# Rotary query columns of four heads in one tile, in a two-layer hybrid decoder kernel

## The chip, the cores and the metric

The kernel runs on one core of one Trainium2 chip. The metric is device time in microseconds (us), the median of the runs shown; one execution was also recorded by the hardware profiler, and all durations below come from that one. TensorE is written PE, its weight loads PEld, VectorE DVE, ScalarE ACT, GpSimd POOL, and SyncE, which issues most transfers, SP.

## The reference, cut to what matters

Two layers work on a residual stream of 512 tokens by 1024 features. Each projects it into an S5 branch, a multi-head latent attention (MLA), a memory cross-attention, gates and a merge. The change lies in MLA, whose query is built like this:

```
q = (_rms_norm(c_q, q_norm) @ w_uq).reshape(bsz, s, 8, 64 + 32)
q_nope = q[..., :64]
q_rope = _apply_rope(q[..., 64:], cos, sin)      # t1*cos - t2*sin | t1*sin + t2*cos
k_rope = _apply_rope(k_rope_in[:, :, None, :], cos, sin)[:, :, 0, :]   # one key for all heads
sc = einsum(q_nope, k_nope) + einsum(q_rope, k_rope), scaled by 96 ** -0.5
p = softmax(where(causal, sc, neg));  out = p @ v
```

c_q has 256 features, there are 8 heads, and each head has 64 plain and 32 rotary features, of which the first 16 (t1) are rotated with the last 16 (t2).

## The kernel before, in words

Everything is held transposed, features on the 128 partitions and the 512 tokens along the row. A product of two fp32 operands is three matmuls: each operand is split into a high part rounded to fp32r and the rest (`split_to`, lines 606 to 610: ACT writes the high part, DVE the low one), and `mm3` (lines 97 to 99) adds high by high, high by low and low by high into one PSUM tile. A weight block is loaded by SP, split the same way, and held in a ring of 4. PSUM has three tiles under the tag "mm" for such products, one under "tp" for transposes, two under "sc" for scores.

PE runs in an order written out by hand; generators hand it pieces of work. The other engines each run in order too, with instructions placed by a scheduler. `attention` walks over the heads. For each it makes the next head's inputs (`prepare`), four score tiles of 128 queries (`mla_scores`, each followed by mask, maximum, exponential, sum and scaling on DVE and ACT), and, delayed by four tiles, the values of the head before (`mla_values`: transposes of the probabilities, a copy of them out of PSUM, two matmuls). Between these pieces PE runs "fill": projections, the GLU and merge products that have nothing to do with attention. Each score tile is followed by 2.5 us of the planner's time of other work, taken from the next head's inputs and the fill (`lace` gives each yield of the inputs 1.2 us of fill). The fill of an even head is queued when that head begins; when the queue is empty PE gets none.

Per pair of heads `mla_k` makes the plain keys, and copies the shared rotated key (32 rows) into each head's key tile, on POOL (line 935). Per head `mla_q` (lines 942 to 958) makes one 128-row PSUM tile: 64 plain features, 32 rotary features, and the same 32 again with t1 and t2 exchanged. So a head has 2 x 3 matmuls of 512 columns. Then ACT copies the plain rows out (line 950), DVE multiplies rows 64 to 95 by the cosines, rows 96 to 127 by the signed sines, and adds (lines 951 to 953), and ACT and DVE split the 96 rows (lines 609, 610). The scores contract over 96 rows.

The cosine table is made in layer 0 during the first merges (`rope_tables`, `v_sincos`), turned by four transposes on PE (line 360) and copied out of PSUM by DVE (line 361). `rotary_sums` and `rotate_key` rotate the shared key right behind it, and in layer 1 at the start of the layer.

Of the kernel before, what the change touches and what calls it, by code (L numbers as in the profile page):

```python
# [230 lines left out]
def const_setup(E):  # L231
# [7 lines left out]
    g.tensor_tensor(out=E.sel[:, 0:32], in0=E.ident[:, 0:32], in1=E.ident[:, 32:64], op=ALU.add)
    for o in (64, 96):  # L240
        g.tensor_tensor(out=E.sel[:, 0:32], in0=E.sel[:, 0:32], in1=E.ident[:, o:o + 32], op=ALU.add)
    g.tensor_copy(E.sel[:, 32:48], E.sel[:, 16:32])
    g.tensor_copy(E.sel[:, 48:64], E.sel[:, 0:16])
# [92 lines left out]
def rope_tables(E):  # L336

    nc, cst = E.nc, E.cst
    v = nc.vector
# [8 lines left out]
    rt = R("rt", 512).rearrange("p (t f) -> p t f", t=4)  # L348
    s3 = rsn.rearrange("p (t f) -> p t f", t=4)
    c3 = rcs.rearrange("p (t f) -> p t f", t=4)  # L350
    for o in range(0, 128, 64):
        v.tensor_copy(rt[:, :, o:o + 16], c3)
        v.tensor_copy(rt[:, :, o + 16:o + 32], c3)
        v.tensor_scalar(out=rt[:, :, o + 32:o + 48], in0=s3, scalar1=-1.0, scalar2=None, op0=ALU.mult)
        v.tensor_copy(rt[:, :, o + 48:o + 64], s3)
# [1139 lines left out]
```

## Time and profile before

| | |
|---|---|
| median of 3 runs | 1108.19 us (1103.96, 1108.19, 1113.60) |
| the profiled execution, its own time | 1108.54 us |
| its span, first to last instruction | 1106.6 us |
| granted PE clock, mean over the span | 0.99 |
| PE / PEld busy | 95% / 77% |
| DVE / ACT / POOL busy | 63% / 46% / 45% |
| share of the last chain: PE / DVE / DMA / ACT / issue | 73% / 11% / 6% / 4% / 4% |

A matmul's listed length reaches past the start of the next one, because matmuls overlap; what a matmul takes out of PE's time is the distance from its start to the next start. A number in brackets at a row's end is the idle time of that engine before it, and what ended it. Layer 0's MLA stretch is 296 to 460 us, layer 1's 830 to 990 us.

### The profile page before, as it was taken

To read this page: it belongs to the slowest core of one execution; us is meant where nothing else is said; L and a number is where in the kernel's file an instruction comes from. 1 tells how busy PE (TensorE), PEld (TensorE's weight loads), DVE (VectorE), ACT (ScalarE), POOL (GpSimd) and SP (SyncE) were. 2 spreads that over 40 slices of the span, in tenths; PEclk is the share of its full clock that TensorE was granted. 3 is DMA by queue.
4 is the path that set the end of the run, shared out by engine and by line. 5 is a ranking of instruction groups with operands and counts; after the bars stand their busy time and mean duration, and the time that the engine had idled before them with its cause. 6 is when DMAs were issued, how large, how long until landed. Compare 5 with 4: busy or idle time off the path is not lost.

```text
span 1106.6 us, 16062 instructions
## 1 busy us (share of the span) xinstructions
PE 1054.7 (95%) x5584; PEld 846.8 (77%) x5584; DVE 693.4 (63%) x1275; ACT 509.5 (46%) x1013; POOL 496.2 (45%) x889
## 2 busy tenths in 40 slices
PE   8939998999999999999989999999999999999996
PEld 6638886887876777788878788888888777778885
DVE  7596869747575654764396675864547665545427
ACT  5315553333566665333335356434347656543331
POOL 3998965871042333682570075673002333310163
PEclk9979999999999999999999999999999999999999
DMA  6515243453321222344545344254432212234342
GB/s 200 176 39 134 81 120 94 120 134 103 100 84 51 61 66 67 115 134 131 150 145 165 110 100 119 83 133 111 114 103 88 74 51 69 75 105 133 101 148 77
DMA packets 87666, 117.97 MB, mean 107 GB/s; under 512 B 24097, under 2 KB 36513, under 8 KB 87585
## 3 DMA queue, kind: packets, MB, share of 16 engines
q1 hardware_dynamic: 86944, 114.85, 36.0%
q0 software_dynamic: 640, 2.10, 0.6%
q8 instruction: 44, 0.72, 0.3%
q14 instruction: 38, 0.30, 0.1%
HBM read 107.37 MB, written 9.55 MB: 106 GB/s over the span
## 4 chain that ended last, share of the span: by engine, by line
PE 73%; DVE 11%; DMA 6%; ACT 4%; issue 4%; POOL 1%; SPq 0%; DVEq 0%; ACTq 0%; POOLq 0%
PE mm L97 20%; PE mm L99 20%; PE mm L98 20%; DVE w L607 3%; PE av L990 2%; DMA raw<-in_w_mem_kv 2%; PE tp L982 2%; ACT w L606 1%; PE pb L519 1%; DMA yd<-r 1%; PE py L543 1%; DMA yb<-yd 1%; PE sa L98 1%; DMA raw<-in_xT 1%; PE sa L99 1%
## 5 line engine op out<-in xcount | busy, mean ns | idle before, releaser
L97 PE MATMUL mm<-X,w 128*128 128x512 f32 x740 | 298.0, 403 | 2.3 <-ACT w L606 1.4
L607 DVE TENSOR_TENSOR w<-raw,w 128x512 fp32r<-128x512 f32 (+1 forms) x247 | 216.4, 881 | 122.9 <-ACT w L606 121.6
L99 PE MATMUL mm<-X,w 128*128 128x512 f32 x740 | 289.4, 391 | 0.1
L98 PE MATMUL mm<-X,w 128*128 128x512 f32 x740 | 289.0, 391 | 0.0
L606 ACT CAST w<-raw 128x512 fp32r<-128x512 f32 (+1 forms) x317 | 191.3, 607 | 183.7 <-PE mm L99 80.1
L71 POOL TENSOR_TENSOR w<-raw,w 128x512 fp32r<-128x512 f32 x70 | 92.7, 1326 | 339.6 <-ACT w L606 259.8
L97 PEld LDWEIGHTS mm<-X,w 128*128 128x128 f32 x740 | 139.7, 189 | 32.1 <-issue 2.8
L99 PEld LDWEIGHTS mm<-X,w 128*128 128x128 f32 x740 | 139.0, 188 | 31.1 <-DVE w L607 0.8
L98 PEld LDWEIGHTS mm<-X,w 128*128 128x128 f32 x740 | 139.4, 188 | 26.4 <-DVE X L607 0.2
L99 PE MATMUL mm<-hl,w 128*128 128x512 f32 (+1 forms) x296 | 110.4, 373 | 18.1 <-DVE w L607 18.1
L97 PE MATMUL mm<-hl,w 128*128 128x512 f32 (+1 forms) x296 | 112.0, 378 | 0.2
L98 PE MATMUL mm<-hl,w 128*128 128x512 f32 (+1 forms) x296 | 109.7, 371 | 0.3 <-DVE hl L610 0.3
L99 PEld LDWEIGHTS mm<-hl,w 128*128 128x128 f32 x296 | 56.8, 192 | 28.5 <-DVE w L607 19.3
L97 PEld LDWEIGHTS mm<-hl,w 128*128 128x128 f32 x296 | 57.1, 193 | 9.7 <-DVE z L727 1.1
L98 PEld LDWEIGHTS mm<-hl,w 128*128 128x128 f32 x296 | 56.9, 192 | 9.2 <-DVE hl L610 1.0
L1048 ACT ACTIVATE thg<-mm,bg 128x512 f32<-128x512 f32 x48 | 32.9, 686 | 62.1 <-PE mm L99 61.8
L782 ACT ACTIVATE P<-P,mx 128x256 f32<-128x256 f32 (+2 forms) x96 | 51.1, 542 | 12.2 <-DVE mx L781 12.2
L780 ACT ACTIVATE P<-sa,mx 128x128 f32<-128x128 f32 (+1 forms) x64 | 33.7, 527 | 31.2 <-DVE mx L772 30.6
L1058 DVE SCALAR_TENSOR_TENSOR thg<-thg,mm 128x512 f32<-128x512 f32 x32 | 22.0, 688 | 34.0 <-PE mm L99 33.2
L777 DVE TENSOR_TENSOR sa<-sa,mask 128x128 f32<-128x128 f32 x64 | 19.1, 298 | 35.0 <-PE sa L99 34.3
L935 POOL TENSOR_SCALAR hl<-hl 32x512 fp32r<-32x512 f32 x32 | 21.1, 658 | 43.1 <-PE mm L98 28.5
L71 POOL TENSOR_TENSOR macc<-macc,thg 128x512 f32<-128x512 f32 x16 | 22.5, 1405 | 36.7 <-DVE thg L1058 36.6
(364 smaller groups left out, 1986.2 us busy)
## 6 DMA issues: line engine op xcount, KB each, us to landing
raw<-in_w_in SPq DMA_DIRECT2D x188, 256.0 KB
raw<-in_p SPq DMA_DIRECT2D x48, 256.0 KB
raw<-in_w_mem_kv SPq DMA_DIRECT2D x32, 256.0 KB
raw<-in_w_out SPq DMA_DIRECT2D x32, 256.0 KB
tz<-kd SPq DMA_DIRECT2D x8, 512.0 KB
raw<-in_w_glu SPq DMA_DIRECT2D x16, 256.0 KB
raw<-in_xT SPq DMA_DIRECT2D x8, 256.0 KB
raw<-in_memT SPq DMA_DIRECT2D x8, 256.0 KB
```

The source lines that it names most:

```text
L71: ins = g.tensor_tensor(**k)
L97: t.matmul(out, lhsT=a[0], rhs=b[0], start=start, stop=False)
L98: t.matmul(out, lhsT=a[0], rhs=b[1], start=False, stop=False)
L99: t.matmul(out, lhsT=a[1], rhs=b[0], start=False, stop=stop)
L606: nc.scalar.copy(hi, src)
L607: (eng or nc.vector).tensor_tensor(out=lo, in0=src, in1=fl(hi), op=ALU.subtract)
L780: nc.scalar.activation(out=P, in_=ps, func=AF.Exp, bias=mx[:, 1:2], accum_out=mx[:, 2:3])
L782: nc.scalar.activation(out=P, in_=P, func=AF.Copy, scale=mx[:, 3:4])
L982: nc.tensor.transpose(tp[:, cols(t)], Ps[t][:, cols(kb)], E.ident)
L990: mm = lambda out, rhs, start, stop: nc.tensor.matmul(out, lhsT=w, rhs=rhs, start=start, stop=stop)
L1048: nc.scalar.activation(out=th, in_=pg, func=AF.Tanh, bias=E.bg2[:, col:col + 1], scale=0.5)
L1058: v.scalar_tensor_tensor(out=th, in0=th, scalar=1.0, in1=pp, op0=ALU.add, op1=ALU.mult)
```

## The change

The doubled 32 columns per head go. The columns of `w_uq` are ordered anew: for four heads (a "quad") one tile of 128 rotary rows, t1 of heads a and b, t2 of heads a and b, then the same for c and d; and for each pair of heads one tile of 2 x 64 plain rows. So a quad has 3 tiles where it had 4, and `mla_q_rope` and `mla_q` run 18 matmuls where 24 ran. A score tile now contracts over 128 rows: 64 plain rows of the head and the 64 rotary rows of its pair, and the key tile holds the shared rotated key at the rows of that head and zeros at the rows of the other (`sel` is 128 columns wide for that).

`rope` rotates on DVE: four products of 32 rows by the sines, read crosswise, one product of 128 rows by the cosines, and one sum of 64 rows per pair. It yields four times, so that fill comes between. `mla_q` then makes both heads of a pair at once: each head's plain rows are split from PSUM, the pair's rotary rows are split once for the first head, and ACT copies the two parts into the second head's tiles. `mla_k` copies the key's rotary rows on ACT for the first head and on POOL for the second. The tables are now two, cosines and sines, each turned by four transposes; the single "tp" tile serves both.

```diff
-    E.sel = cst.tile([128, 64], F32, name="sel")
+    E.sel = cst.tile([128, 128], F32, name="sel")
...
 def rope_tables(E):
...
-    E.cs = cst.tile([128, 512], F32, name="cs", tag="cs")
-    tp = E.psum.tile([128, 512], F32, name="tp", tag="tp", bufs=E.cfg["tp"])
-    for t in range(4):
-        nc.tensor.transpose(tp[:, t * 128:t * 128 + 128], rt[:, t, :], E.ident)
-    nc.vector.tensor_copy(E.cs, tp)
+    E.cs = []
+    for r, tag in ((rc, "cs"), (rs, "sin")):
+        tp = E.psum.tile([128, 512], F32, name="tp", tag="tp", bufs=E.cfg["tp"])
+        for t in range(4):
+            nc.tensor.transpose(tp[:, t * 128:t * 128 + 128], r[:, t * 128:t * 128 + 128], E.ident)
+        E.cs.append(cst.tile([128, 512], F32, name="cs", tag=tag))
+        nc.vector.tensor_copy(E.cs[-1], tp)
...
+def rope(E, a, b, ps, outs):
+    v = E.nc.vector
+    cos, sin = E.cs
+    for o in (0, 32, 64, 96):
+        i = o ^ 32
+        v.tensor_tensor(out=b[o:o + 32, :], in0=ps[i:i + 32, :], in1=sin[i:i + 32, :], op=ALU.mult)
+        if o == 32:
+            yield
+    yield
+    v.tensor_tensor(out=a, in0=ps, in1=cos, op=ALU.mult)
+    for r, out in outs:
+        v.tensor_tensor(out=out, in0=a[r, :], in1=b[r, :], op=ALU.add)
+        yield
...
         for i in range(2):
-            nc.gpsimd.tensor_scalar(out=k[i][64:96, :], in0=fl(E.kr[i][64:96, :]), scalar1=1.0, scalar2=0.0,
-                                    op0=ALU.mult, op1=ALU.add)
+            if j:
+                nc.gpsimd.tensor_scalar(out=k[i][64:128, :], in0=fl(E.kr[i][64:128, :]), scalar1=1.0, scalar2=0.0,
+                                        op0=ALU.mult, op1=ALU.add)
+            else:
+                nc.scalar.copy(k[i][64:128, :], fl(E.kr[i][0:64, :]))
...
-def mla_q(E, l, hp, j, wq):
-    pq = pmm(E)
-    for k in range(2):
-        mm3(E, pq, wq.at(cols(2 * j + k)), E.cn[k].at(ALL), k == 0, k == 1)
-    qf, tb = ftile(E, "qf"), ftile(E, "qb")
-    nc.scalar.copy(qf[0:64, :], pq[0:64, :])
-    v.tensor_tensor(out=qf[64:96, :], in0=pq[64:96, :], in1=E.cs[64:96, :], op=ALU.mult)
-    v.tensor_tensor(out=tb[64:96, :], in0=pq[96:128, :], in1=E.cs[96:128, :], op=ALU.mult)
-    v.tensor_tensor(out=qf[64:96, :], in0=qf[64:96, :], in1=tb[64:96, :], op=ALU.add)
-    q = ftile2(E, "A")
-    split_to(E, q[0][0:96, :], q[1][0:96, :], qf[0:96, :], 96 ** -0.5)
-    yield
+def mla_q_rope(E, l, hq):
+    w = wblock(E, E.I["w_uq"][l, hq, :, 0:512])
+    pq = pmm(E)
+    for k in range(2):
+        mm3(E, pq, w.at(cols(k)), E.cn[k].at(ALL), k == 0, k == 1)
+    r = [stile(E, "qr") for _ in range(2)]
+    yield from rope(E, ftile(E, "qa"), ftile(E, "qb"), pq, [(cols(i, 64), r[i][64:128, :]) for i in range(2)])
+    return [(r[0], w), (r[1], None)]
+
+def mla_q(E, l, hp, qr, wq):
+    o = 2 if wq else 0
+    wq = wq or wblock(E, E.I["w_uq"][l, hp // 2, :, 512:768], 256)
+    pq = pmm(E)
+    for k in range(2):
+        mm3(E, pq, wq.at(cols(o + k)), E.cn[k].at(ALL), k == 0, k == 1)
+    qs = [ftile2(E, "A") for _ in range(2)]
+    r = slice(64, 128)
+    for j, q in enumerate(qs):
+        split_to(E, q[0][0:64, :], q[1][0:64, :], pq[cols(j, 64), :], 96 ** -0.5)
+        if j == 0:
+            split_to(E, q[0][r, :], q[1][r, :], qr[r, :], 96 ** -0.5)
+            yield
+        else:
+            for i in range(2):
+                nc.scalar.copy(q[i][r, :], fl(qs[0][i][r, :]))
...
         if j == 0:
             ks[hp] = yield from mla_k(E, l, hp)
-            ws[hp] = wblock(E, E.I["w_uq"][l, hp])
-        qs[h] = yield from mla_q(E, l, hp, j, ws[hp])
+            if h % 4 == 0:
+                ws[hp], ws[hp + 1] = yield from mla_q_rope(E, l, h // 4)
+            qs[h], qs[h + 1] = yield from mla_q(E, l, hp, *ws[hp])
```

The written order moves at three places that the prediction speaks of. In the rows, "waits X" says on which engine's signal an instruction waits.

First, PE in layer 0 where the tables are turned (`ident` is the unit matrix, `carve` the tables, `ks`, `sel` the shared key). Before:

```order
L894 MATMUL mm<-ks,sel 64x512 [waits DVE_49]
L360 MATMUL tp<-ident,carve 128x128 x4
L97 MATMUL mm<-X,w 128x512 [waits Activation_49]
L98 MATMUL mm<-X,w 128x512
L99 MATMUL mm<-X,w 128x512 [waits DVE_49]
```

And now:

```order
L899 MATMUL mm<-ks,sel 128x512 [waits DVE_49]
L363 MATMUL tp<-ident,carve 128x128 x4
L363 MATMUL tp<-ident,carve 128x128 [waits DVE_49]
L363 MATMUL tp<-ident,carve 128x128 x3
L97 MATMUL mm<-X,w 128x512 [waits Activation_49]
```

Four more transposes stand there, and the first of them waits for DVE, which has to copy the first four out of the one "tp" tile. On DVE that copy keeps its place, behind the scan (line 531 before) and four more instructions.

Second, DVE of the changed kernel where the fifth head's first score tile comes near (`sa` are scores, `mx` the softmax's columns, `qr` rotary rows, `hl<-mm` the plain rows of the query):

```order
L781 TENSOR_TENSOR sa<-sa,mask 128x128 [waits PE_49]
L611 TENSOR_TENSOR w<-raw,w 128x512 [waits DMAHW6_49,Activation_49]
L776 TENSOR_REDUCE mx<-sa 128x1 [waits DVE_49]
L614 SCALAR_TENSOR_TENSOR hl<-qr,hl 64x512 [waits Activation_49]
L785 RECIPROCAL mx<-mx 128x1 [waits Activation_49]
L614 SCALAR_TENSOR_TENSOR hl<-mm,hl 64x512 [waits Activation_49]
L611 TENSOR_TENSOR w<-raw,w 128x512 [waits DMAHW7_49,Activation_49]
L781 TENSOR_TENSOR sa<-sa,mask 128x128 [waits PE_49]
```

The query's last piece, `hl<-mm`, stands behind the reciprocal of the softmax of the fourth head's last tile. On PE its six matmuls now come right behind that score tile, and six matmuls of fill later the fifth head's first score tile needs them; before, a head's six matmuls stood three score tiles or more ahead of their use.

Third, PE in layer 1 at the end of the second head. Before:

```order
L97 MATMUL sa<-hl 128x512 [waits DVE_49]
L990 MATMUL av<-pt,vv 64x128 [waits Activation_49]
L982 MATMUL tp<-ident,P 128x128 [waits PE_49]
L97 MATMUL mm<-ysm,w 128x512
L98 MATMUL mm<-ysm,w 128x512
L99 MATMUL mm<-ysm,w 128x512 [waits Pool_49]
...
L97 MATMUL sa<-hl 128x128 [waits Activation_49]
L982 MATMUL tp<-ident,P 128x128 [waits Activation_49]
```

And now:

```order
L97 MATMUL sa<-hl 128x512 [waits Activation_49]
L1026 MATMUL av<-pt,vv 64x128 [waits Activation_49]
L1018 MATMUL tp<-ident,P 128x128 [waits PE_49]
L97 MATMUL sa<-hl 128x128 [waits Activation_49]
L1018 MATMUL tp<-ident,P 128x128 [waits Activation_49]
```

The twelve matmuls of fill between the two score tiles are gone from here; the four yields of `rope` have used the fill earlier. Layer 0 had no fill at this point already. At the end of each MLA stretch, too, one block of twelve fill matmuls between the last head's transposes is gone.

## Rows read from the trace of the kernel before

**Rows 1.** The page, part 1: busy time, share of the span, instructions.
```profile
PE 1054.7 (95%) x5584; PEld 846.8 (77%) x5584; DVE 693.4 (63%) x1275; ACT 509.5 (46%) x1013; POOL 496.2 (45%) x889
```
**Rows 2.** Waits of PE: engine, line, releaser; us in total, times, longest.
```profile
PE mm L99 <- DVE w L607: 18.1, 5, 12.2
PE tp L982 <- ACT P L782: 4.7, 4, 2.6
PE av L990 <- ACT pt L985: 3.5, 8, 0.7
PE tx L1123 <- DVE mv L181: 3.2, 1, 3.2
```
**Rows 3.** Timeline of PE, first and last of 38 even matmuls: start, length.
```profile
295.65 0.39 PE L98 MATMUL mm<-hl,w 128*128 128x512 f32 x1
304.04 0.39 PE L99 MATMUL mm<-hl,w 128*128 128x512 f32 x1
```
**Rows 4.** Timeline of PE at the turning of the table.
```profile
252.72 0.66 PE L360 MATMUL tp<-ident,carve 128*128 128x128 f32 x4
253.13 0.49 PE L97 MATMUL mm<-X,w 128*128 128x512 f32 x1
```
**Rows 5.** Timeline of DVE at the same place.
```profile
252.95 1.22 DVE L531 TENSOR_TENSOR_SCAN pb<-r,pb 128x512 f32<-128x512 f32 x1
...
256.21 0.69 DVE L361 COPY cs<-tp 128x512 f32<-128x512 f32 x1
```
**Rows 6.** Timeline of PE: the longer early waits.
```profile
60.80 0.58 PE L99 MATMUL mm<-hl,w 128*128 128x256 f32 x1 [4.66 <-DVE w L607]
80.40 0.58 PE L99 MATMUL mm<-hl,w 128*128 128x256 f32 x1 [12.19 <-DVE w L607]
```
**Rows 7.** Stretches: length, busy PE, PEld, DVE, ACT, POOL, then PE's granted clock.
```profile
60.00:62.00 2.00, 1.20 (x5) 1.20 (x6) 2.00 (x2) 0.00 (x0) 2.00 (x8) 0.63 0.16 25
62.00:64.00 2.00, 1.73 (x9) 1.44 (x7) 2.00 (x1) 0.59 (x1) 2.00 (x9) 0.52 0.32 107
572.00:574.00 2.00, 0.13 (x1) 0.14 (x2) 1.98 (x7) 1.71 (x4) 1.96 (x3) 1.00 0.00 0
345.00:400.00 55.00, 53.97 (x280) 40.53 (x279) 33.17 (x74) 33.00 (x77) 19.15 (x30) 1.00 0.22 64
```
**Rows 8.** Timeline of DVE, then of PE, at layer 0's first heads.
```profile
304.66 0.69 DVE L951 TENSOR_TENSOR qf<-mm,cs 32x512 f32<-32x512 f32 x1
...
310.99 1.46 DVE L1035 TENSOR_TENSOR gl<-gl,z 128x512 f32<-128x512 f32 x1
308.47 0.22 PE L97 MATMUL sa<-hl 96*128 96x128 f32 x1
324.76 0.33 PE L982 MATMUL tp<-ident,P 128*128 128x128 f32 x1 [2.59 <-ACT P L782]
```
**Rows 9.** Timeline of PE, end of the second head: layer 0, layer 1.
```profile
341.83 0.33 PE L982 MATMUL tp<-ident,P 128*128 128x128 f32 x1 [1.65 <-ACT P L782]
872.75 0.66 PE L982 MATMUL tp<-ident,P 128*128 128x128 f32 x4
```
**Rows 10.** Softmax of one 512-column score tile, on DVE and ACT.
```profile
322.26 0.68 DVE L772 TENSOR_REDUCE mx<-sa 128x1 f32<-128x512 f32 x1
322.98 0.69 ACT L780 ACTIVATE P<-sa,mx 128x512 f32<-128x512 f32 x1 [0.84 <-DVE mx L772]
```
**Rows 11.** Timeline of PE: the last head's uncovered copy in layer 0.
```profile
455.54 0.43 PE L990 MATMUL av<-pt,vv 128*64 128x128 f32 x2 [0.36 <-ACT pt L985]
```
**Rows 12.** Groups of instructions by line: busy us, mean ns, idle before.
```profile
L950 ACT COPY qf<-mm 64x512 f32<-64x512 f32 x16 | 9.3, 579 | 5.9 <-PE mm L99 5.8
L609 ACT ACTIVATE hl<-qf 96x512 fp32r<-96x512 f32 x16 | 10.1, 629 | 11.8 <-DVE qf L953 11.6
L951 DVE TENSOR_TENSOR qf<-mm,cs 32x512 f32<-32x512 f32 x16 | 11.0, 689 | 5.9 <-ACT qf L950 5.6
L777 DVE TENSOR_TENSOR sa<-sa,mask 128x128 f32<-128x128 f32 x64 | 19.1, 298 | 35.0 <-PE sa L99 34.3
```

More of the change, by code (lines that the diff above doesn't have):

```diff
@@ L236, in const_setup @@
     make_identity(nc, E.ident)
-    E.sel = cst.tile([128, 64], F32, name="sel")
+    E.sel = cst.tile([128, 128], F32, name="sel")
     g = nc.gpsimd
[L239 to L243, printed above, removed]
+    g.memset(E.sel, 0.0)
+    for a, b in ((0, 0), (32, 16)):
+        d = E.sel[:, a:a + 16]
+        g.tensor_tensor(out=d, in0=E.ident[:, b:b + 16], in1=E.ident[:, b + 32:b + 48], op=ALU.add)
+        for o in (64, 96):
+            g.tensor_tensor(out=d, in0=d, in1=E.ident[:, b + o:b + o + 16], op=ALU.add)
+        g.tensor_copy(E.sel[:, a + 80:a + 96], d)
     E.sp = cst.tile([128, 1], F32, name="sp")
@@ L249, in const_setup @@
     v.memset(E.sn[64:128, :], -1.0)
-    E.ones = E.cst.tile([128, 32], F32, name="ones")
+    E.ones = E.cst.tile([128, 1], F32, name="ones")
     v.memset(E.ones, 1.0)
@@ L277, in load_params @@
     nc.sync.dma_start(out=E.pos, in_=E.I["pos"])
-    E.bg2 = E.cst.tile([128, 48], F32, name="bg2")
+    E.bg2 = E.bgate
     v.tensor_scalar(out=E.bg2, in0=E.bgate, scalar1=0.5, scalar2=None, op0=ALU.mult)
@@ L347, in rope_tables @@
     yield from v_sincos(nc, v, pr, rsn, rcs, rang, 64)
[L348 to L355, printed above, removed]
[L356 to L361 removed]
+    rc, rs = R("rc", 512), R("rs", 512)
+    by16 = lambda a, n: a.rearrange("p (t o f) -> p t o f", t=4, o=1).to_broadcast([128, 4, n, 16])
+    v.tensor_copy(rc.rearrange("p (t r f) -> p t r f", t=4, r=8), by16(rcs, 8))
+    for o in range(0, 8, 4):
+        r4 = rs.rearrange("p (t r f) -> p t r f", t=4, r=8)
+        v.tensor_copy(r4[:, :, o:o + 2, :], by16(rsn, 2))
+        v.tensor_scalar(out=r4[:, :, o + 2:o + 4, :], in0=by16(rsn, 2), scalar1=-1.0, scalar2=None, op0=ALU.mult)
+    yield
+    E.cs = []
[5 more added lines that the diff above has]
+        nc.vector.tensor_copy(E.cs[-1], tp)
 def s5_powers(E, l):
@@ L845, in latents @@
         for t in range(4):
-            nc.tensor.matmul(ss[32 * t:32 * t + 32, cols(j)], lhsT=E.ones, rhs=sq[2 * j][:, cols(t)], start=True, stop=True)
+            nc.tensor.matmul(ss[32 * t:32 * t + 32, cols(j)], lhsT=E.ones.to_broadcast([128, 32]), rhs=sq[2 * j][:, cols(t)], start=True, stop=True)
     m2, hu = stile(E, "ms"), stile(E, "hu")
@@ L893, in rotary_sums @@
     ps = pmm(E)
-    E.nc.tensor.matmul(ps[64:128, :], lhsT=E.sel, rhs=E.ks, start=True, stop=True)
+    E.nc.tensor.matmul(ps, lhsT=E.sel, rhs=E.ks, start=True, stop=True)
     return ps
+def rope(E, a, b, ps, outs):
[11 more added lines that the diff above has]
+        yield
 def rotate_key(E, ps):
-    v = E.nc.vector
     a, b = stile(E, "ka"), stile(E, "kb")
-    v.tensor_tensor(out=a[64:96, :], in0=ps[64:96, :], in1=E.cs[64:96, :], op=ALU.mult)
-    v.tensor_tensor(out=b[64:96, :], in0=ps[96:128, :], in1=E.cs[96:128, :], op=ALU.mult)
-    v.tensor_tensor(out=a[64:96, :], in0=a[64:96, :], in1=b[64:96, :], op=ALU.add)
+    drain(rope(E, a, b, ps, [(cols(0), a)]))
     E.kr = ftile2(E, "A")
-    split_to(E, E.kr[0][64:96, :], E.kr[1][64:96, :], a[64:96, :])
+    split_to(E, *E.kr, a)
 def mla_v(E, l, i):
@@ L1454, in pack @@
     cols = []
-    for h in range(8):
-        q = list(range(h * 96, h * 96 + 96))
-        cols += q + q[80:] + q[64:80]
+    for hq in range(2):
+        h = [list(range(i * 96, i * 96 + 96)) for i in range(4 * hq, 4 * hq + 4)]
+        for a, b in (h[0:2], h[2:4]):
+            cols += a[64:80] + b[64:80] + a[80:] + b[80:]
+        for a in h:
+            cols += a[0:64]
     w = f("w_uq")[:, :, cols]
-    A["w_uq"] = w.reshape(DEPTH, 2, 128, 4, 2, 128).transpose(0, 3, 2, 4, 1, 5).reshape(DEPTH, 4, 128, 512)
+    A["w_uq"] = w.reshape(DEPTH, 2, 128, 2, 3, 128).transpose(0, 3, 2, 4, 1, 5).reshape(DEPTH, 2, 128, 768)
     w = f("w_ukv").reshape(DEPTH, 128, 8, 2, 64)
```

10 lines of the change are left out of this document (4 added, 6 removed).

## The prediction

> **What bounds the kernel now.** I read the busy shares first, then what PE waits for, then PE's own timeline, and last the stretches in which the change lies. PE is busy 95% of the span, DVE 63%, ACT 46% [rows 1]. All waits of PE of any size come to some 30 us: 18.1 us lie in the first 81 us, where DVE is late with weights, and behind the scores only 4.7 us (scaled probabilities) and 3.5 us (copies of their transposes) are lost in the whole kernel [rows 2]. So a matmul that goes away shortens the kernel by its start-to-start distance, and an instruction on DVE, ACT or POOL costs only where PE stands behind it. That distance: 37 steps take 304.04 - 295.65 = 8.39 us, 0.227 us each [rows 3]; the listed 0.39 us overlaps the next matmul and is not the price. The sum starts from the profiled execution's 1108.54 us, 0.35 us above the median of the runs shown.
>
> **The matmuls that go.** Per layer two quads, each 18 matmuls instead of 24: 24 fewer in all, 24 x 0.227 = **-5.4 us**. The score matmuls contract over 128 rows instead of 96; their columns stay, so I charge nothing.
>
> **The second table.** Four more transposes: four took 253.13 - 252.72 = 0.41 us [rows 4], **+0.4 us**. But between the two groups PE now waits until DVE has copied the first out of the single "tp" tile. Before, PE went on to a projection at 253.13, and nobody on PE waited for that copy; it began at 256.21, because DVE worked through a scan from 252.95 on and three more instructions first, and took 0.69 us [rows 5]. With DVE's order ahead of it unchanged, PE resumes at 256.9: 256.90 - 253.13 = **+3.8 us**. If DVE happened to be free, it would be the copy alone, 0.7 us; that is the low end. DVE's second copy and the five products and sums of the shared key keep their distance to PE: weights for the next products are split up to a ring of four ahead.
>
> Would the clock fall in this wait? [...]
>
> **Layer 0's first scores.** The rotary rows of four heads are now finished before the first score tile, not those of one. DVE reached the first rotary product at 304.66 [rows 8], held up by work that stays. From there its new order has four sine products, a cosine product, two sums, two GLU steps and two splits before the first head's query is whole: 11 x 0.69 us [rows 12] = 7.6 us, so 312.3. PE would want it earlier: its last matmul of the rotary tile ends where the first head's query ended before, at about 302.9; then follow 18 matmuls of fill (4.1), 6 of the query (1.4) and the values' 12 half-width ones (1.4), 309.8. That is a wait of 2.5 us; with a GLU step stretched as one was, 1.46 instead of 0.69 us [rows 8], 3.3 us. Against it, DVE has one instruction for the second head's query between the following score tiles instead of four, 3 x 0.69 = 2.1 us less, so the 2.59 us that PE waited for the first head's probabilities at 324.76 [rows 8] should fall to about 0.7, -1.9 us. Net **+0.6 us**, between -1 and +3.
>
> **Fill that is used up earlier.** In layer 0 the second head ended without fill already, and PE waited 1.65 us for the probabilities there; in layer 1 twelve matmuls covered it, and there was no wait [rows 9]. Now layer 1 lacks them too: **+1.7 us** (0.5 to 3). At the end of both stretches one copy of transposed probabilities loses its twelve matmuls. The one that was uncovered cost 0.36 us [rows 11]; with a larger copy I take 0.5 each, **+1.0 us** (0.6 to 1.3).
>
> **The fifth head's query, in both layers.** From the fourth head's last score tile on: two value matmuls and a transpose (0.3 us), six query matmuls (1.4), six of fill (1.4), then the fifth head's scores at 3.1 us. DVE goes mask 0.30, weights 0.69, maximum 0.68, rotary split 0.69 to about 2.4 us, then must wait for ACT's exponential (0.69 us [rows 10], and 0.2 for its sum) before the reciprocal at 2.9, and only then does the split of the plain rows start, behind ACT's own 0.6 us [rows 12] that follow the exponential: done at 4.1 us. PE waits 1.0 us, **+2.0 us** in both layers (0 to 4: PE may lag, or weights come late in this queue).
>
> **Relief and load elsewhere.** Per quad DVE loses three instructions (16 become 13), POOL half its key copies; ACT gets 14 where it had 8, six of about 0.6 us [rows 12]. DVE's 2 us less per quad should take something off the 8.2 us that PE waits behind the softmax [rows 2]: **-1.0 us** (0 to -3). ACT is busy 33 of 55 us in such a stretch [rows 7]; I charge its extra 3.6 us per quad at nothing, hidden in its 40% idle time, and price the loss of that cover as a rival.
>
> **Sum.** -5.4 + 0.4 + 3.8 + 0.6 + 1.7 + 1.0 + 2.0 - 1.0 = +3.1: 1111.6 us against the profiled execution, 1111.3 against the median. Forecast **1111 us**, no change that a measurement of this kernel can tell (about 1%, 11 us).
>
> **Rivals.**
> *The waits are covered.* If DVE is free at the table (0.7 instead of 3.8) and of the other waits only the low 0.6 us at the ends of the stretches is left, it is -5.4 + 0.4 + 0.7 + 0.6 - 1.0 = -4.7: 1104 us. For it: PE loses only 8.2 us behind the softmax now. Against it: two of the waits stand in the written order, whatever the engines do. Chance 0.25.
> *The clock falls at the table wait.* [...] For it the clock behind the 4.66 us wait, against it the 3.2 us wait [rows 6, 7]. Chance 0.13.
> *ACT becomes the bound in the MLA stretch (slower).* ACT's queue is in order, and the 24 extra casts of query and key halves stand between exponentials, scalings and copies of transposes. If each delays the piece that PE needs next, all 24 x 0.6 = 14.4 us reach PE: with -5.4, +0.4, +3.8 and +1.0 at the stretch's end 1108.5 + 14.2 = 1123 us. It decides once ACT has no idle time in front of PE's waits. Against it the 40% idle time, and that these casts have their data early. Chance 0.08.
> *The early weights wait moves.* 18.1 us of PE's waiting lie in the first 81 us [rows 2, 6]; no instruction there changes its place, apart from nine small POOL ones for `sel` instead of five at the very start. Were it gone: 1091 us. Chance 0.04.
> The forecast itself 0.50.
>
> **Range and chances.** Low end: -5.4 + 0.4 + 0.7 - 1 + 0.5 + 0.6 + 0 - 3 = -7.2, 1101 us. High end: -5.4 + 0.4 + 3.8 + 1.7 + 3 + 3 + 1.3 + 4 = +11.8, 1120 us. I give 1101 to 1119, which leaves out the early wait, most of the ACT case, and the edges. Over 1% faster, under 1097: 0.05 (the early wait, and a little of the covered case). Over 1% slower, over 1119: 0.10 (the ACT case and the forecast's upper edge). Within 1%: 0.85.
>
> **What would show it.** In the changed kernel's trace: 24 fewer matmul records; a PE wait of some 3.8 us for DVE between two groups of four transposes at about 253, and the clock behind it; a wait of some 2 to 3 us at layer 0's first score matmul; a new wait of 1 to 2 us at the end of layer 1's second head; one of about 1 us at the fifth head's first score in each layer. If the waits behind the softmax grew from 8 to over 15 us, ACT would be the cause. If the time fell by about 5 us with none of these waits, I have misread what DVE does ahead of them.

## The result, and the profile after

The changed kernel takes **1123.71 us** (median of 4 runs, 1123.17 to 1124.85), the kernel before 1107.1 us (4 runs, 1103.96 to 1113.6): ratio **1.0138, interval 1.0105 to 1.0172**, slower by 1.4%. The prediction said 1111 us, between 1101 and 1119: it was wrong. The profiled execution after took 1123.56 us (span 1121.4), 15 us more than the one before.

The page's busy row, and PE's granted clock in 40 slices:

```profile
PE 1059.7 (94%) x5564; PEld 849.9 (76%) x5564; DVE 692.8 (62%) x1267; ACT 524.9 (47%) x1037; POOL 488.8 (44%) x877
...
PEclk9979999999999999999999999999999899999999
```

PE has 20 instructions fewer (24 matmuls gone, 4 transposes more) and is yet busy 5.0 us longer than in [rows 1]: busy time that grows while work shrinks points at the clock. Stretches of the trace (columns as in [rows 7]), the first over nearly the whole kernel before, the others after:

```profile
90.00:1095.00 1005.00, 986.69 (x5232) 793.92 (x5231) 615.56 (x1132) 475.60 (x955) 423.55 (x693) 1.00 0.36 104
```
```profile
246.30:249.70 3.40, 3.40 (x9) 2.64 (x9) 2.42 (x3) 1.09 (x3) 3.32 (x5) 0.52 0.35 73
324.80:328.20 3.40, 3.40 (x11) 2.73 (x10) 0.64 (x3) 2.05 (x6) 1.31 (x2) 0.52 0.03 8
355.50:358.90 3.40, 3.40 (x12) 2.83 (x12) 0.12 (x1) 0.59 (x1) 0.00 (x0) 0.51 0.02 5
584.20:587.60 3.40, 3.39 (x11) 2.88 (x12) 3.19 (x10) 1.73 (x3) 2.18 (x4) 0.52 0.57 163
888.00:894.80 6.80, 5.97 (x22) 5.35 (x22) 1.18 (x3) 1.99 (x6) 0.00 (x0) 0.51 0.13 39
```

Before, PE ran at full clock (1.00) from 90 us on. After, it was granted 0.51 or 0.52 five times, 4 x 3.4 + 6.8 = 20.4 us, in which about half the work is done: **10.2 us lost** at most. Such a stretch at half clock is called a fall below. Each of the five stands behind a wait, or begins inside it. PE's timeline at two of them, layer 0's first score and the end of layer 1's second head (start, length, instruction; in brackets the idle time and its releaser):

```profile
319.47 0.27 PE L98 MATMUL sa<-hl 128*128 128x128 f32 x1
323.31 0.33 PE L99 MATMUL sa<-hl 128*128 128x128 f32 x1 [3.56 <-DVE hl L614]
...
324.45 0.42 PE L98 MATMUL mm<-X,w 128*128 128x512 f32 x1
324.68 0.62 PE L99 MATMUL mm<-X,w 128*128 128x512 f32 x1
325.10 0.63 PE L97 MATMUL mm<-X,w 128*128 128x512 f32 x1
...
885.84 0.43 PE L1026 MATMUL av<-pt,vv 128*64 128x128 f32 x2 [0.63 <-ACT pt L1021]
...
888.83 0.48 PE L1018 MATMUL tp<-ident,P 128*128 128x128 f32 x1 [2.08 <-ACT P L786]
...
890.38 0.63 PE L97 MATMUL mm<-X,w 128*128 128x512 f32 x1
890.81 0.63 PE L98 MATMUL mm<-X,w 128*128 128x512 f32 x1
```

From start to start a matmul takes 0.42 us there, not the 0.23 of [rows 3].

These are two single executions, and the one of the kernel before had lost little to the clock. Its granted clock, mean over the span, was 0.990; in 35 later executions of the same kernel it was 0.980 to 0.991, median 0.985, and in the eight of the changed kernel 0.975 to 0.983. Taken as (1 - clock) x span, which counts half clock during waits too, the traced execution before lost 11 us, a usual one some 17, and the two sets of four after 22 and 26 (medians). So, as an estimate from these numbers, the clock makes 5 to 8 of the 15 to 17 us between the medians, and longer waits make the rest; the 10.2 us hold for this pair of traces.

The waits of PE after, and one row of those before:

```profile
PE mm L99 <- DVE w L611: 16.8, 4, 12.2
PE tp L507 <- ACT bmT L508: 5.6, 4, 2.3
PE tp L1018 <- ACT P L786: 4.2, 2, 2.1
PE sa L99 <- DVE hl L614: 4.1, 3, 3.6
...
PE av L1026 <- ACT pt L1021: 2.9, 6, 0.6
PE tp L363 <- DVE cs L365: 2.7, 1, 2.7
PE tx L1159 <- DVE mv L181: 2.4, 1, 2.4
```
```profile
PE tp L503 <- ACT bmT L504: 1.4, 3, 0.6
```

The waits behind the softmax did not grow (4.7 + 3.5 in [rows 2], 4.2 + 2.9 now). They are fewer and longer: 2.08 us, with 0.64 just ahead, at the end of the second head in each layer. New are 3.56 us at the first score, 2.70 at the table, and at 245 us a longer wait for a copy on ACT (bmT: 2.33 us, before 0.42), which stands in ACT's queue behind the landing of a transfer, issued at 235.54 us before and at 237.35 after (ACT's timeline, before and after):

```profile
239.62 1.19 ACT L609 ACTIVATE hl<-yb 128x512 fp32r<-128x512 f32 x1 [4.22 <-DMA yb<-yd]
```
```profile
243.31 1.12 ACT L613 ACTIVATE hl<-yb 128x512 fp32r<-128x512 f32 x1 [6.21 <-DMA yb<-yd]
```

Laying the same instructions of both traces beside each other tells where the 15.1 us arise (start after minus start before, at PE):

| stretch, us after | offset grows by | made of |
|---|---|---|
| 0 to 240 | 1.7 | put down to landings of early transfers, not taken apart |
| 240 to 250 | 3.5 | 1.9 longer wait for bmT, 1.7 clock |
| 250 to 262 | 3.0 | 2.7 wait at the table, 0.4 transposes |
| 262 to 520 | 2.2 | matmuls -2.7, waits +1.7, clock +3.4 |
| 520 to 800 | 1.7 | clock +1.7, waits for bmT +2.0, tx -0.8, rest -1.2 |
| 800 to 1002 | 3.0 | matmuls -2.7, waits +2.4, clock +3.4 |

In sum: matmuls -5.4, transposes +0.4, clock +10.2, waits and landings +9.9.

### The profile page after: what moved, and what is told of

It is laid out like the page before. It is cut to its first block, busy times and chain, and to the rows that moved or that the text cites. A ratio compares the mean times of both kernels' runs of the same rounds, so it can differ in the third digit from the quotient of the medians.

```text
span 1121.4 us, 16019 instructions
## 1 busy us (share of the span) xinstructions
PE 1059.7 (94%) x5564; PEld 849.9 (76%) x5564; DVE 692.8 (62%) x1267; ACT 524.9 (47%) x1037; POOL 488.8 (44%) x877
## 4 chain that ended last, share of the span: by engine, by line
PE 72%; DVE 13%; DMA 8%; ACT 3%; issue 3%; POOL 1%; SPq 0%; DVEq 0%; ACTq 0%; POOLq 0%
PE mm L97 19%; PE mm L99 19%; PE mm L98 19%; DVE w L611 3%; PE av L1026 2%; DMA yb<-yd 2%; PE tp L1018 2%; DMA yd<-r 2%; DMA raw<-in_w_mem_kv 2%; PE py L547 1%; PE pb L523 1%; DVE qb L910 1%; ACT w L610 1%; DVE hl L614 1%; DMA raw<-in_xT 1%
## 5 line engine op out<-in xcount | busy, mean ns | idle before, releaser
L611 DVE TENSOR_TENSOR w<-raw,w 128x512 fp32r<-128x512 f32 (+2 forms) x247 | 214.2, 873 | 110.8 <-ACT w L610 109.8
L99 PE MATMUL mm<-hl,w 128*128 128x512 f32 (+1 forms) x288 | 107.0, 372 | 16.8 <-DVE w L611 16.8
L97 PE MATMUL mm<-hl,w 128*128 128x512 f32 (+1 forms) x288 | 108.4, 376 | 0.4 <-DVE hl L611 0.4
L98 PE MATMUL mm<-hl,w 128*128 128x512 f32 (+1 forms) x288 | 106.4, 370 | 0.5 <-DVE hl L614 0.5
L99 PEld LDWEIGHTS mm<-hl,w 128*128 128x128 f32 x288 | 55.3, 192 | 26.7 <-DVE w L611 17.7
L1084 ACT ACTIVATE thg<-mm,par 128x512 f32<-128x512 f32 x48 | 33.0, 688 | 65.4 <-PE mm L99 65.1
L97 PEld LDWEIGHTS mm<-hl,w 128*128 128x128 f32 x288 | 55.6, 193 | 9.8 <-PE mm L99 0.7
L98 PEld LDWEIGHTS mm<-hl,w 128*128 128x128 f32 x288 | 55.5, 193 | 9.1 <-DVE hl L614 1.0
L785 DVE RECIPROCAL mx<-mx 128x1 f32<-128x1 f32 x96 | 15.4, 160 | 40.3 <-ACT P L784 39.2
```

What stands on the lines that cost most here:

```text
L97: t.matmul(out, lhsT=a[0], rhs=b[0], start=start, stop=False)
L98: t.matmul(out, lhsT=a[0], rhs=b[1], start=False, stop=False)
L99: t.matmul(out, lhsT=a[1], rhs=b[0], start=False, stop=stop)
L611: (eng or nc.vector).tensor_tensor(out=lo, in0=src, in1=fl(hi), op=ALU.subtract)
L1084: nc.scalar.activation(out=th, in_=pg, func=AF.Tanh, bias=E.bg2[:, col:col + 1], scale=0.5)
```

## Experiments

Where not said otherwise, the base is the changed kernel. The profiled executions are up to 5.5 us apart already at the issue of yb's transfer, ahead of the places edited here (233.5 us with work in the waits, 239.0 with two table tiles), so besides medians I compare stretches: the distance between the same two matmuls, minus that distance in the changed kernel's trace.

| kernel | median us | ratio to before | 240 to 300 | 300 to 520 | 520 to 800 | 800 to 1002 |
|---|---|---|---|---|---|---|
| before | 1107.1 to 1110.5 | 1 | -7.3 | -1.4 | -1.7 | -3.0 |
| busy waits | 1117.6 | 1.0082 (1.0055 to 1.011) | +0.5 | -3.1 | +1.1 | -2.7 |
| copies on POOL | 1120.88 | 1.009 (1.0057 to 1.0123) | +1.9 | -3.0 | +0.8 | -4.4 |
| two table tiles | 1122.32 | 1.0115 (1.0067 to 1.0163) | -1.5 | +0.9 | +0.6 | 0.0 |
| third GLU tile as fill | 1118.62 | 1.0082 (1.0051 to 1.0113) | +1.3 | -1.5 | -0.1 | -4.4 |
| fill spread | 1121.74 | 1.0105 (1.0075 to 1.0136) | +0.7 | -1.2 | +0.4 | -3.1 |
| table copies on ACT | 1116.68 | 1.0064 (1.0039 to 1.0089) | -3.4 | +0.7 | -0.1 | -0.2 |
| five edits | 1104.85 | **0.9958 (0.9944 to 0.9972)** | -5.8 | -6.6 | +1.0 | -5.4 |
| changed kernel again | 1126.37 | 1.0141 (1.0101 to 1.0182) | +0.6 | 0.0 | +1.9 | -1.2 |

The changed kernel itself stands at 1123.71 us, 1.0138 (1.0105 to 1.0172). Only "table copies on ACT" and "five edits" have an interval wholly below that one; the other edits are judged by their stretches, each read from one execution. The last row shows how far such a stretch moves with nothing changed: up to 0.6 us ahead of 520 us, up to 1.9 behind it.

### Work for PE in the waits

```
+ def keep_busy(E, ps, n):
+     z = E.ident.bitcast(BF16)
+     for _ in range(n):
+         E.nc.tensor.matmul(ps[:, 0:256], lhsT=z[:, 0:128], rhs=z[:, 0:256], start=True, stop=True)
...
+             keep_busy(E, ps, busy)    # busy: 28 at layer 0's first score; 18 or 20 at the other four places
```

> Edit: the changed kernel, with independent bf16 matmuls of 256 columns (the identity tile as both operands) ahead of five places at which TensorE waited in its trace: 18 ahead of the last group of bm transposes of layer 0 (waited 2.33 us), 20 between the two groups of table transposes (2.70), 28 ahead of layer 0's first score (3.56), 18 ahead of the second head's last transposes in each layer (2.08 each), 20 ahead of the second group of tx transposes (2.44). Nothing else is computed or moved; no wait of another engine changes. [...] Rival B (only the length of the waits counts, the clock is a side effect that the next wait absorbs): 1122 to 1125 us, as the changed kernel. Rival C (ACT is late everywhere): no change either, 1123 us.

Measured: 1117.6 us, 6 us less than the changed kernel, of the 10.2 that the falls had cost at most. PE at the first score and at the end of layer 0's second head, then the stretch behind the first score, whose granted clock (1.00) stands third from the end:

```profile
315.66 3.23 PE L687 MATMUL sa<-ident 128*128 128x256 bf16 x28
...
319.62 0.33 PE L99 MATMUL sa<-hl 128*128 128x128 f32 x1 [0.56 <-DVE hl L618]
...
346.64 2.14 PE L687 MATMUL tp<-ident 128*128 128x256 bf16 x18
348.62 0.49 PE L1037 MATMUL tp<-ident,P 128*128 128x128 f32 x3
```
```profile
320.00:327.00 7.00, 7.00 (x34) 5.88 (x34) 3.46 (x11) 5.26 (x13) 1.33 (x2) 1.00 0.20 56
```

What PE waits for comes no earlier, but the falls behind the first score and both second heads' ends are gone: the stretches around them got 1.6, 1.6 and 2.6 us shorter, 5.8 in all, where half clock alone had cost 1.7 + 1.7 + 3.4 = 6.8. So the clock costs time of its own, and rival B falls for these places. At bmT the fall is gone too (1.00 from 243 to 247 us), but yb landed earlier in this execution, so that place tells nothing. Two places failed. At tx the added matmuls themselves waited 2.82 us for their PSUM slot and the clock fell there as before (0.72 from 574 to 580 us). At the table PE waited 2.61 us behind the added matmuls: there DVE sets the time, see below.

### ACT's copies on POOL

```
-            if j:
-                nc.gpsimd.tensor_scalar(out=k[i][64:128, :], in0=fl(E.kr[i][64:128, :]), ...)
-            else:
-                nc.scalar.copy(k[i][64:128, :], fl(E.kr[i][0:64, :]))
+            r = (0, 64)[j]
+            nc.gpsimd.tensor_scalar(out=k[i][64:128, :], in0=fl(E.kr[i][r:r + 64, :]), ...)
...
-                nc.scalar.copy(q[i][r, :], fl(qs[0][i][r, :]))
+                nc.gpsimd.tensor_scalar(out=q[i][r, :], in0=fl(qs[0][i][r, :]), ...)
```

> Edit: the changed kernel, with the copies that the change gave to ACT (both halves of the first head's rotary key rows per pair, and both halves of the odd head's rotary query rows; 16 per layer, 32 in all) on POOL. Rival C (ACT's extra casts reach TensorE, 14.4 us, the prediction's slower rival at 1123 us): most of that comes back, 1110 to 1113 us. Theory A (clock falls behind waits that ACT's copies do not cause): 1121 to 1126 us, with the waits at layer 0's first score (3.56 us), at the table (2.70) and at the second heads' ends (2.08) still there; POOL takes more than 1 us for such an instruction, so that a late key may even cost 1 to 3 us.

Measured: 1120.88 us. Groups of POOL, then PE at the end of layer 0's second head:

```profile
L955 POOL TENSOR_SCALAR hl<-hl 64x512 fp32r<-64x512 f32 x32 | 21.4, 674 | 52.0 <-PE mm L98 30.1 <-ACT hl L610 19.6 <-DVE hl L611 0.6
L990 POOL TENSOR_SCALAR hl<-hl 64x512 fp32r<-64x512 f32 x16 | 10.9, 680 | 4.5 <-ACT hl L613 2.3 <-DVE hl L614 1.2
```
```profile
351.89 0.33 PE L1017 MATMUL tp<-ident,P 128*128 128x128 f32 x1 [1.33 <-ACT P L786]
```

Both theories missed. The wait at each second head's end went from 0.64 + 2.08 to 0.07 + 1.33 us, and no fall stands behind it any more (in layer 1 the clock is 1.00 from 805 to 996 us): -3.0 and -4.4 us in the two MLA stretches, 7.4 in all; the waits make 2.6 of it, the two falls up to 5.1. So ACT's copies did reach PE, at one place per layer, with a fifth of the rival's 14.4 us; the fall behind it cost more than the wait. POOL took 0.68 us, not over 1. The +1.9 us from 240 to 300 us is the table: PE waited 5.77 us there in this execution, and the clock fell for 6.8 us.

### The tables' transposes in two tiles

```
-        tp = E.psum.tile([128, 512], F32, name="tp", tag="tp", bufs=E.cfg["tp"])
+        tp = E.psum.tile([128, 512], F32, name="tr", tag="sc")
```

> Edit: the changed kernel, with the two groups of table transposes in two PSUM tiles of the score ring, which is idle there, so that the second group has not to wait for DVE's copy of the first. Theory A: the wait of 2.70 us goes; no fall of the clock stood behind it, so 2.7 us and no more come back: 1121 us (1119 to 1122.5; a fall of the clock elsewhere may come or go with the shift, 1.7 us each). Rival D (the wait moves to the next reader of the tables, the shared key's rotation, and from there to the first scores): 1123.5 us.

Measured: 1122.32 us. The wait between the groups is gone, but PE waits further on. PE, then DVE:

```profile
256.67 1.04 PE L363 MATMUL tr<-ident,carve 128*128 128x128 f32 x8
...
269.96 0.50 PE L99 MATMUL mm<-X,w 128*128 128x512 f32 x1 [3.63 <-DVE w L611]
```
```profile
262.13 0.69 DVE L365 COPY cs<-tr 128x512 f32<-128x512 f32 x1
...
263.34 0.68 DVE L365 COPY cs<-tr 128x512 f32<-128x512 f32 x1
...
264.62 2.79 DVE L910 TENSOR_TENSOR kb<-mm,cs 32x512 f32<-32x512 f32 x4
267.42 0.69 DVE L914 TENSOR_TENSOR ka<-mm,cs 128x512 f32<-128x512 f32 x1
...
268.63 0.68 DVE L916 TENSOR_TENSOR ka<-ka,kb 128x512 f32<-128x512 f32 x1
269.23 1.28 DVE L611 TENSOR_TENSOR w<-raw,w 128x512 fp32r<-128x512 f32 x2
```

From 256 to 262 us it gained 2.9, up to 300 us it lost 3.9 again. (The -1.5 in the table holds another -2.5 us ahead of 250 us, where the wait for bmT was 1.46 us.) Rival D: the split of PE's next weights stands behind both copies and the shared key's rotation on DVE, which the change made longer, six instructions instead of three. The prediction counted five and held them to be covered by weights split ahead.

### The third GLU tile as fill

```
-            run(E, chain(*[glu_tile(E, l, i, z[i]) for i in range(3)]))
-            mla_phase(E, l, glu_tile(E, l, 3, z[3]), ...
+            run(E, chain(*[glu_tile(E, l, i, z[i]) for i in range(2)]))
+            mla_phase(E, l, chain(*[glu_tile(E, l, i, z[i]) for i in (2, 3)]), ...
```

> Edit: the changed kernel, with the third GLU tile (24 matmuls) taken out of the block ahead of the MLA phase and put ahead of the fourth in the phase's fill; so the four-head rotary matmuls stand 24 matmuls (5.4 us) earlier on TensorE, and DVE has that much longer until the first score. Nothing is added or left out. Theory A: layer 0's wait at the first score (3.56 us, with the 0.35 us ahead of it) goes, and with it the fall of the clock at 325 us (1.7 us): 1123.7 - 5.3 = 1118.4 us (1117 to 1121); the waits at the second heads' ends stay, since the fill is used up as before. Rival B (the wait alone): 1120 us, with the clock still falling there. Rival E (DVE reaches the rotary products late because of other work, not because of TensorE's order): the wait stays, 1123 us.

Measured: 1118.62 us. The wait at the first score and its fall are gone (-5.2 us from 319 to 328 us, as expected). Part comes back at the first head's probabilities:

```profile
338.50 0.33 PE L1018 MATMUL tp<-ident,P 128*128 128x128 f32 x1 [2.20 <-ACT P L786]
```

The second head's end in layer 0 kept its wait and fall. In layer 1 that wait was 1.33 us, without a fall, which I had not expected of this edit. At the table PE waited 4.70 us, with a fall of 6.8 us (granted clock 0.79 from 254 to 263 us). Theory A holds for the first score alone; that the median came out where it said, 1118.4, is in part luck, since 2 us came back at the first heads and the 4.4 us of layer 1 were not forecast.

### The fill spread over the first two heads

```
-            advance(E, f, us)
+            advance(E, f, 1.9 if lace_us and h < 2 else us)
```

> Edit: the changed kernel, with 9 fill matmuls behind each score tile of the first two heads of the MLA phase instead of 12 (1.9 us of planned time instead of 2.5), so that the same fill reaches to the end of the second head. Nothing is added or left out. Theory A (the second head's end stands without fill, PE waits 0.64 + 2.08 us there in each layer, and the clock falls behind it for 3.4 us in layer 0 and 6.8 us in layer 1): the two waits go down by some 2 us per layer and both falls go: -2 - 1.7 from 300 to 465 us, -2 - 3.4 from 850 to 1002 us, 9 us in all, 1114.6 us (1112 to 1118). Rival B (the softmax of the first two heads then has too little behind it, and PE waits for it three matmuls earlier at each tile): as much lost as won, 1122 to 1125 us.

Measured: 1121.74 us; -1.2 us from 300 to 520 us, -3.1 from 800 to 1002: 4.3, half of what was expected. PE at the ends of the first and second heads in layer 0, and the stretch behind the second, at a granted clock of 1.00:

```profile
337.59 0.33 PE L1018 MATMUL tp<-ident,P 128*128 128x128 f32 x1 [0.97 <-ACT P L786]
...
353.03 0.33 PE L1018 MATMUL tp<-ident,P 128*128 128x128 f32 x1 [1.47 <-ACT P L786]
```
```profile
353.00:360.00 7.00, 6.97 (x41) 5.75 (x42) 3.65 (x10) 4.45 (x12) 2.26 (x3) 1.00 0.21 60
```

One wait of 2.72 us has become two, 0.97 and 1.47. All waits of PE from 300 to 520 and from 800 to 1005 us come to 12.6 us with the edit and 12.4 without: in length nothing is won, as rival B said. But the falls behind both second heads' ends are gone, 5.1 us of lost clock, and that is what the edit won. This is the clearest separation of the two costs.

At the table PE waited 4.70 us here and the clock fell for 3.4, as with the third GLU tile as fill. In both, and with the copies on POOL, the wait for bmT was 1.27 to 1.49 us instead of 2.33; PE came to the table sooner and waited longer there, since DVE's copy stood behind a weight split for which ACT waited 2.77 to 3.83 us until the weight had landed. From 240 to 263 us these three took 0.7 to 1.9 us longer than the changed kernel. So the 2.70 us at the table, and the clock that did not fall there, came with the long wait for bmT ahead of it; the two losses do not simply add.

### The tables' copies on ACT

```
-        nc.vector.tensor_copy(E.cs[-1], tp)
+        nc.scalar.copy(E.cs[-1], tp)
```

> Edit: the changed kernel, with both copies of the rotary tables out of PSUM on ACT instead of DVE. Theory A2 (DVE is the bound of the stretch from 250 to 300 us, so that a wait taken off one place comes back at another, as when the second group had a tile of its own: -2.9 us at the table, +3.9 us up to 300 us, where TensorE waited 3.6 us for a weight split that stood behind the shared key's rotation on DVE): two of DVE's instructions of 0.69 us go, and the copy no longer waits for a scan: the wait between the groups falls from 2.7 to about 0.9 us and does not come back in full, so the stretch from 250 to 300 us gets 1 to 3 us shorter: 1121 to 1123 us. Rival D (the first copy's wait alone): -1.8 us at the table, nothing lost behind it. Rival F (weights from DMA come late there, whatever the engines do): the stretch stays as long as in the changed kernel.

Measured: 1116.68 us, below the expected 1121 to 1123; -3.4 us from 240 to 300 us, and the wait is still 2.12, not 0.9:

```profile
254.03 0.33 PE L363 MATMUL tp<-ident,carve 128*128 128x128 f32 x1 [2.12 <-ACT cs L365]
```

Of the 3.4 us, 2.8 lie ahead of 250 us, where the wait for bmT was 1.12 us without a fall (a landing, not this edit); 0.6 us are the edit's. The profiled execution is another 3.6 us ahead by 240 us, where weights landed earlier; how much of the median comes from that is not known. So the single tile and DVE are both in the way, and to take away one gains little; the next kernel takes both away.

### Five edits at once

> Edit: the changed kernel with five edits at once: the 32 key and query copies of ACT on POOL, the tables' transposes in two tiles of the score ring and their copies on ACT, the third GLU tile as fill ahead of the first scores, and 9 instead of 12 fill matmuls behind the first two heads' score tiles. Theory A (the changed kernel lost by some 10 us of half clock and some 10 us of new waits, each at a place that one of these edits covers): of the 15 us against the kernel before, first score and its fall 5.3, second heads' ends with their falls 8, table 2 go, which leaves the matmuls' -5.4: between 1104 and 1110 us, at or just under the kernel before. Rival B (the waits are a budget: DVE and ACT owe the same work and give it back elsewhere): 1116 to 1122 us.

Measured: **1104.85 us, ratio 0.9958 (0.9944 to 0.9972)**: faster than the kernel before, and 1.8% under the changed kernel. Its largest waits, then the stretch at the table:

```profile
PE mm L99 <- DVE w L611: 16.9, 4, 12.2
PE tp L507 <- ACT bmT L508: 5.2, 4, 1.5
PE tp L1017 <- ACT P L786: 3.4, 4, 1.2
```
```profile
254.00:262.00 8.00, 8.00 (x40) 6.57 (x39) 6.17 (x9) 3.94 (x7) 0.00 (x0) 1.00 0.30 92
```

PE does not stop at the table, no wait of the MLA stretches is over 1.22 us, and from 90 us to the last matmul the clock falls once, for 3.4 us at tx (0.66 from 572 to 577 us).

### The changed kernel again

> The changed kernel once more, unchanged, beside the three edits on the same chip, to see which of its waits and falls of the clock come back. Theory A: the waits at layer 0's first score (3.6 us), at the second heads' ends (2.1 us each) and at the table recur, since the written order makes them; falls of the clock stand behind most of them, not always the same; 1119 to 1125 us. The wait for a DMA at 243 us (2.3 us) and the length of the early wait for weights (12.2 us) may change, since a transfer's landing sets them.

Measured: 1126.37 us, just above the expected 1125. PE's waits of the changed kernel come back to within 0.1 us at the places that the order makes, and that for bmT too:

```profile
246.70 0.55 PE L507 MATMUL tp<-ident,bm 128*128 128x128 f32 x3 [2.38 <-ACT bmT L508]
...
325.10 0.33 PE L99 MATMUL sa<-hl 128*128 128x128 f32 x1 [3.60 <-DVE hl L614]
...
356.35 0.33 PE L1018 MATMUL tp<-ident,P 128*128 128x128 f32 x1 [2.08 <-ACT P L786]
...
892.51 0.48 PE L1018 MATMUL tp<-ident,P 128*128 128x128 f32 x1 [2.07 <-ACT P L786]
```

Falls stand behind the same five waits, and one more at 189 us behind one of 3.02 us, which in the first trace, at 2.96, had none. The lengths differ: at tx PE waited 3.63 us, not 2.44, with 6.8 us at half clock and not 3.4, and at the end of layer 1's second head the fall was 3.4 us and not 6.8. So the places come back, and the price of one fall does not to within 1.7 us.

### The edits of order on the kernel before

The same two diffs as for the third GLU tile and the spread fill.

> Edit: the kernel before, with the two edits of order alone: the third GLU tile as fill ahead of the first scores, and 9 instead of 12 fill matmuls behind the score tiles of the MLA phase's first two heads. Theory A: the kernel before waited 2.59 us at 324.76 and 1.65 us at 341.83, with no fall of the clock behind either, and nothing of that kind in layer 1; what there is to win is at most those 4.2 us, so 1105 to 1109 us: the repaired changed kernel (1104.9) leads by its 24 matmuls and not by the order. Rival G (the order is what won, and the change itself is worth nothing): 1102 to 1104 us, level with the repaired changed kernel or ahead of it.

Measured: 1121.83 us, ratio 1.0113 (1.0084 to 1.0141). Both expectations missed: they make the kernel before **slower** by 11 us. PE in layers 0 and 1, then the stretch in layer 1:

```profile
319.56 0.47 PE L982 MATMUL tp<-ident,P 128*128 128x128 f32 x1 [2.65 <-ACT P L782]
...
328.76 0.47 PE L97 MATMUL mm<-ysm,w 128*128 128x512 f32 x1 [2.52 <-DVE hl L607]
...
860.61 0.77 PE L97 MATMUL mm<-hl,w 128*128 128x512 f32 x1 [3.65 <-DVE hl L607]
```
```profile
858.80:869.00 10.20, 7.13 (x19) 4.57 (x20) 4.64 (x9) 2.97 (x6) 1.40 (x3) 0.51 0.08 23
```

The wait for the first head's probabilities is as long as before (2.59 us, [rows 8]) but now has a fall; the waits of 2.52 and 3.65 us for DVE are new, each with a fall: 17 us at half clock in the two stretches. Rival G falls: the order that suits the changed kernel does not suit this one. What each of the two edits did was not taken apart.

### The 24 matmuls put back

```
+    for k in range(2):
+        mm3(E, pq, w.at(cols(k)), E.cn[k].at(ALL), True, True)
     for k in range(2):
         mm3(E, pq, w.at(cols(k)), E.cn[k].at(ALL), k == 0, k == 1)
```

> Edit: the repaired changed kernel (five edits at once), with the six rotary matmuls of each quad issued once ahead of the real ones into the same PSUM tile, which overwrite them: 24 needless matmuls, nothing else. The prediction's first term: 24 x 0.227 = 5.4 us more, 1104.85 + 5.4 = 1110.3 us (1109 to 1112). Rival H (the matmuls only fill time in which TensorE would wait for DVE and ACT): 1105 to 1107 us.

Measured: 1108.7 us, 3.9 above the kernel with five edits, 2.1 by the ratios (0.9977, 0.9962 to 0.9993, against 0.9958): below the expected 1109 to 1112, above rival H's 1105 to 1107 by the median. In the traces PE falls behind by 1.3 and 1.4 us at the second quad of the two layers, where 6 x 0.227 = 1.4 was expected. At the first quads it is level again within 17 us, because waits of 0.62 and 0.36 us (layer 0) and 0.62 and 0.25 us (layer 1), which followed there, went instead. That makes 2.7 us. The prediction's first term holds at its price where PE has no wait behind it, at two quads of four; at the other two rival H is right.

## Why the prediction was wrong

Its named terms, with what the traces show:

| term | predicted | measured |
|---|---|---|
| 24 matmuls | -5.4 | -5.4 by count; 2.7 where put back into the kernel with five edits |
| four transposes | +0.4 | +0.4 |
| wait at the table | +3.8 | +2.7 |
| layer 0's first scores | +0.6 | +1.3 (0.35 + 3.56 waited, 2.59 gone) |
| second head's end, layer 1 | +1.7 | +2.7 |
| second head's end, layer 0 | 0 | +1.1 (1.65 to 2.72) |
| tails | +1.0 | +0.9 |
| fifth head | +2.0 | +1.0 |
| relief of other softmax waits | -1.0 | -3.3 |
| sum | +3.1 | +1.4 |

Within 2.3 us the named waits were read rightly, each at its place. **The step that failed is the clock.** The prediction asked "Would the clock fall in this wait?" of the table alone, put 0 into the sum and 1.7 us into the high end. The 1.7 us is what the clock lost behind the early wait of 4.66 us, 2 x 0.37 + 2 x 0.48 [rows 6, 7]; the 0 goes by the wait of 3.2 us at 572, inside which the clock was 1.00, since 3.8 us is nearer to it. It did not ask of the first score, which it put at 2.5 to 3.3 us itself, nor of the second heads' ends. Behind those three the clock fell to 0.51 or 0.52 for 3.4, 3.4 and 6.8 us, 1.7 us for each 3.4: 6.8 us lost, three times the +0.6 and +1.7 that the sum had for these places. The work put into the waits (5.8 us back) and the spread fill (4.3 us) show that this is a cost of its own. Two more falls (245 us, 584 us), 3.4 us, stand behind waits for bmT and tx that the change does not touch.

The 0 for the table held at 258 to 262 us after, where the clock stayed at 1.00, but by luck: where PE waited 4.70, 4.70 and 5.77 us there, in three variants, it fell. The row on which the 0 rests was an exception too. It is the tx wait of 3.21 us, read inside the wait [rows 7]; behind that same wait a fall stands at 2.44 us in the changed kernel, at 2.89 with the 24 matmuls put back, at 3.0 with five edits and at 3.80 with the edits of order on the kernel before.

A second term put at nothing was ACT's 3.6 us more per quad, "hidden in its 40% idle time". With these copies on POOL the second heads' waits fell from 2.72 to 1.40 us in each layer, and the falls behind them went; with the third GLU tile as fill layer 1's wait was 1.40 us with the copies on ACT too, so they reach PE only at some timings. And "all waits of PE of any size", put at 30 us, come to 41 in the trace before: left out were 3.0 us at 188 us and the 1.4 us for bmT, which grew.

The remaining error is mostly landings: the transfer of yb took 4.1 us from issue to its reader before and 6.0 after (bmT wait +1.9), later bmT waits +2.0, and, as far as they are landings, the 1.7 us ahead of 240 us. In the profiled executions of the changed kernel and its variants it took 4.5 to 6.0 us, in the two of the kernel before and its variant 4.1. Why is **open**: no experiment took it apart.

The rivals. *ACT becomes the bound* gave 1123 us, the number measured, by a mechanism that did not happen: its 14.4 us were to come as waits behind the softmax, and those fell from 8.2 to 7.1 us. With the copies on POOL 7.4 us came back, some two thirds of it clock. *The clock falls at the table wait* named the right cause, once instead of five times, and at a place where it did not happen in this kernel's two traces. *The waits are covered* was refuted by the trace, and *the early weights wait* did not move (18.1 to 16.8 us).

The score matmuls, charged at nothing for their 32 more rows, took no longer than before: from start to start 0.23 us over 128 rows and 512 columns, 0.24 over 96 rows (layer 0, medians).

What the change is worth: with its waits covered 1104.85 us, some 0.4% (4 us) under the kernel before, for 5.4 us of matmuls. The kernel before was not improved likewise, since the two edits tried on it made it slower; a part of the lead may be order and clock (mean granted clock 0.9865 against 0.984) and not matmuls.

## What to carry to other kernels

Ask of every wait you forecast on PE, not of the longest alone, what the clock does behind it, and carry 1.7 us or more for it in the range (3.4 us at 0.51 or 0.52 behind four of the five waits here, 6.8 behind one); splitting a wait of 2.7 us in two, in both layers, won 4.3 us here (3.1 against the changed kernel's second trace) though PE waited as long. Here the operands of four heads were finished together, and their cost came as one long wait at the first use (3.56 us) and as fill used up early (2.08 us waited at the end of each second head), so move independent matmuls to such places and see whether another engine can take the copies; the order has to be found for each kernel, since what helped here cost the kernel before 11 us. The wait of 2.70 us at the table, taken away in a stretch that DVE bounds, came back as one of 3.63 us for DVE, which ended 13 us behind the start of the transposes: compare the whole stretch.

## What the runs showed of the hardware

- The length of a wait alone did not decide the fall. The clearest case is one wait for rb at 184 to 190 us: 3.02 us before and 2.96 us in the first trace of the changed kernel, with the clock at 1.00 behind both, and 3.02 us in the second trace of the changed kernel, with a fall.
- No fall stood behind waits of 1.33 us (copies on POOL), 1.47 (fill spread) and 1.65 (before) at a second head's end. A fall stood behind each of 1.85, 2.33 and 2.38 us for bmT (24 matmuls put back, the changed kernel twice), behind 2.72 us at the changed kernel's second heads' ends, and behind 3.56 and 3.60 us at its first score. Behind 2.59 (first head, before), 2.70 (table), 3.21 (tx, before) and 3.63 us (weights, tables in two tiles) the clock did not fall; behind 2.65 us at that same first head, with the edits of order, it did, to 0.52.
- bf16 matmuls of 256 columns on the identity, results unread, kept the granted clock at 1.00 (318 to 322, 346 to 352 and 878 to 888 us) through the waits at the first score and the second heads' ends, which had been 2.1 to 3.6 us long (28 took 3.23 us).
- POOL's copy of 64x512 took 0.68 us (copies on POOL), ACT's 0.62 (the changed kernel).
